# The FFN inputs of a hybrid decoder layer: how their background work is cut into stages

## The chip, the cores and the metric

The kernel is one program on one core of a Trainium2 chip. The metric is the device time in microseconds. Before the change the median of three runs is 2029.3 us (2027.58 to 2030.84).

## The reference, cut to what matters

One layer, 2048 tokens, width 1024, float32:

```
h = rmsnorm(x, norm_mix) * (1 + sc_m) + sh_m
proj = h @ w_in                      # conv mixer and gated mixer, 512 channels each
x = x + g_m * (y_mix @ w_out)        # "out_proj"

h = rmsnorm(x, norm_ffn) * (1 + sc_f) + sh_f       # the FFN inputs
gate, up = split(h @ w_up, 2)        # 1024 -> 2 x 2816
x = x + g_f * ((silu(gate) * up) @ w_down)
y = rmsnorm(x, norm_final)
```

The change concerns the second `h` alone, that is how and when it is computed.

## The kernel before, in words

Channels lie on the 128 partitions and tokens along the rows. The 2048 tokens are four quarters of 512; two quarters make a half, b = 0 or 1. A float32 product is three matmuls on TensorE (PE): each operand is split into a high and a low part, by a copy on ScalarE (ACT, L151) and a subtraction on VectorE (DVE, L152).

Order of the work: half 0 through both mixers and out_proj; half 1 through the convolution mixer (`restart`), the gated mixer (`mixer`) and out_proj; then the FFN's up projection for half 0 and half 1 (`ups`); then the down projection (`down`).

Both FFN projections use a scheme with seven products in place of eight on 2x2 blocks. The right operands of the up projection are therefore not `h` but seven arrays: B11, B21, B22 (quarters and halves of the channels of `h`), and the differences T1 = B12 - B11, T2 = B22 - T1, T3 = T2 - B11, T4 = B21 - T2. `ffn_inputs(b)` makes them in the background of other work, in four passes over kt (128 channels each, from the first and the second half of the channels). It is a generator: each `next()` runs it to its next `yield`, and whoever calls `next()` decides where its instructions stand in the program. A pass reads four tiles of x from DRAM (`xd`), multiplies each by the reciprocal root mean square on GpSimd (POOL, L478), applies gain and shift on ACT (L479, in place), forms four differences on POOL (L494, L500, L506, L508), and stores seven tiles to DRAM (`hd`, L465). A store is put on a list and issued by the next `late.flush()`, behind the latest weight load on the DMA queue. All DMAs are issued by SyncE (SP), in order.

Background work of half 0 runs under `restart` and `mixer` of half 1 (`step()` there is a `next()`), of half 1 under `ups` for half 0. Under `ups` for half 1 the background is `down_sums`, which is not changed.

`ups` walks over 11 pairs of column tiles for each half. A pair has seven products in the order P1, P5, P6, P2, P7, P3, P4 (k = 0 to 6), each of two units of 12 matmuls, so 24 matmuls. After product k the program makes one of the next pair's weights (`weights`: DMA `raw_gu`, POOL differences L595, L596, L599, L604, then the split of A or ws), at k = 0 the POOL sums of the pair before (L678, L680), at k = 3 and k = 5 its stores (L674) with the differences L686 and L687, and in the slots k = 2 and k = 5 one `next()` of the background. The PSUM bank `a` of a unit is used by P1 (copied out by ACT, `s` L628), P6 (`u` L628), P7 (added to `c` by DVE, L647) and P4, each of which begins when the one before has been read out. `s` is then finished after P2 by a sum on DVE (L643) and Silu on ACT (L644).

The background of half 0's `ups` begins with `finish_rms` (eight matmul records `ms` on PE, L146, and the reciprocal root on ACT and DVE), which needs the last squares of out_proj (`sq`, L439), and goes on with `ffn_inputs(1)`.

What the program's order means: a planner orders the instructions of each engine ahead of time, by its own estimate of durations, the earlier in the program first where several are ready. On the chip each engine runs its list in that order, and an instruction that waits holds all that stand behind it on its engine. The pool of [128, 512] tiles (`tmp`) has 17 slots, shared by all of this.

Of the kernel before, what the change touches and what calls it, by code (L numbers as in the profile page):

```python
# [42 lines left out]
def trunk_kernel(  # L43
# [31 lines left out]
    def panel(name, shape, dt=F32R):  # L75
        return pool.tile(shape, dt, tag="panel", name=name, bufs=14)
# [13 lines left out]
    def tmp(name):  # L90
        return tmx(name)[:, :Q]
# [114 lines left out]
    def more_modulation(n):  # L206
        for _ in range(min(n, len(todo))):
            t = todo.pop(0)
            raw = rawslot(f"wm_{t}")
            nc.sync.dma_start(raw, wmodT[t - 16])  # L210
            modulation(t, raw)
            if 32 <= t < 40:
                gains(1, V_NFFN, t - 32)
# [109 lines left out]
    def token_rms(t, name):  # L323

        n = Q // P
        ms = pool.tile([P, n], F32, tag="ms", name=f"ms_{name}", bufs=1)
        for c in range(n):
            sq = tmp(f"sq_{name}")
            nc.scalar.activation(sq, t[:, c, :], AF.Square, accum_out=ms[:, c:c + 1])
        nc.vector.tensor_scalar_mul(ms, ms, 1.0 / CW)  # L330
        r = pool.tile([P, n], F32, tag="rt", name=f"rt_{name}", bufs=2)
        rsqrt_into(r, ms, n)
        return r

    def token_major(u0, hqs, outs, name, after=lambda kt: None):

        pss = [[ps_tile(f"{name}_{i}_{c}") for c in range(Q // P)] for i in range(len(hqs))]
        for kt in range(KT):
            if kt % 2 == 0:
                ws = halves(u0 + kt // 2, f"{name}_{kt // 2}")  # L340
            w = ws[kt % 2]
            for i, hq in enumerate(hqs):
                for c in range(Q // P):
                    csl = slice(c * P, c * P + P)
                    mm3(pss[i][c], hq[kt][:, 0, csl], hq[kt][:, 1, csl], w[:, 0, :], w[:, 1, :],
                        kt == 0, kt == KT - 1)
            after(kt)
        for i, out in enumerate(outs):
            for c in range(Q // P):
                nc.scalar.activation(out[:, c, :], pss[i][c], AF.Gelu_apprx_tanh)  # L350
# [20 lines left out]
    def channel_major(y, name):  # L371
        out = hi_lo_views(f"yb_{name}", CT)
        for ct in range(CT):
            ps = ps_tile(f"tr_{name}_{ct}")
            for c in range(Q // P):
                csl = slice(c * P, c * P + P)
                nc.tensor.transpose(ps[:, csl], y[:, c, ct * P:ct * P + P], ident)
            scaled_split(out[ct], ps, vcol(V_ONB + ct))
        return out
# [8 lines left out]
    def mixer(b, hT, conv, ws_sb, step):  # L388


        vn = [panel(f"v_{b}_{i}", [P, 4, Q], F32) for i in range(QB)]
        token_major(U_V, hT, vn, f"v{b}", lambda kt: (more_modulation(2), step()))
        for i in range(QB):
            conv.normalise(i)
        for i, v in enumerate(vn):
            r = token_rms(v, f"v{b}_{i}")
            for c in range(Q // P):
                nc.vector.scalar_tensor_tensor(
                    out=v[:, c, :], in0=v[:, c, :], scalar=r[:, c:c + 1], in1=vn_b, op0=ALU.mult, op1=ALU.mult
                )  # L400
        us = [panel(f"u_{b}_{i}", [P, 4, Q], F32) for i in range(QB)]
        y = []
        token_major(U_U, hT[:1], us[:1], f"u{b}_0", lambda kt: (more_modulation(1), step()))
        spatial_gate(us[0], vn[0], ws_sb, f"{b}_0")
        y.append(conv.split(0))

        def after(kt):
            step()
            if kt == 5:
                y[0] += channel_major(us[0], f"{b}_0")  # L410

        token_major(U_U, hT[1:], us[1:], f"u{b}_1", after)
        spatial_gate(us[1], vn[1], ws_sb, f"{b}_1")
        y.append(conv.split(1))
        return y, lambda: channel_major(us[1], f"{b}_1")
# [37 lines left out]
    class Late:  # L453
# [5 lines left out]
        def put(self, dst, t):  # L459
            self.stores.append((dst, t))  # L460
# [7 lines left out]
    def ffn_inputs(b):  # L468

        late = Late()  # L470

        def put(name, kt, t):
            late.put(hd[b][name][:, kt, :], t)

        def get(i, kt):
            t = tmp(f"b_{b}_{i}_{kt}")
            nc.sync.dma_start(t, xd[b][kt // 2][:, 2 * (kt % 2) + i, :])
            nc.gpsimd.tensor_mul(t, t, rs[i])  # L478
            nc.scalar.activation(  # L479
                t, t, AF.Identity, bias=mod[:, 24 + kt:25 + kt], scale=gain[:, 1, kt:kt + 1]  # L480
            )
            return t

        rs = [tmp(f"r_{b}_{i}") for i in range(QB)]
        for i in range(QB):
            nc.sync.dma_start(rs[i], rd[b][i])
        yield
        for kt in range(4):
            b11 = get(0, kt)
            put("B11", kt, b11)  # L490
            t1 = get(1, kt)
            yield
            late.flush()
            nc.gpsimd.tensor_sub(t1, t1, b11)  # L494
            put("T1", kt, t1)
            t2 = get(1, kt + 4)
            put("B22", kt, t2)
            yield
            late.flush()
            nc.gpsimd.tensor_sub(t2, t2, t1)  # L500
            put("T2", kt, t2)
            b21 = get(0, kt + 4)
            put("B21", kt, b21)
            yield
            late.flush()
            nc.gpsimd.tensor_sub(b11, t2, b11)  # L506
            put("T3", kt, b11)
            nc.gpsimd.tensor_sub(b21, b21, t2)  # L508
            put("T4", kt, b21)
            yield  # L510
            late.flush()

    def down_sums():

# [27 lines left out]


    ORDER_UP = ("P1", "P5", "P6", "P2", "P7", "P3", "P4")
    ORDER_DOWN = ("P1", "P6", "P7", "P4", "P5", "P3", "P2")

    class Panel:
# [17 lines left out]
        def steps(self):  # L565
            for p in ORDER_UP:
                self.load(RIGHT[p])
                yield
                self.split(RIGHT[p])
                yield  # L570
# [122 lines left out]
    def ups(panels, begin, backgrounds):  # L693


        todo = [(b, p) for b in range(NB) for p in range(NPR)]
        pair, before = begin, None
        for n, (b, p) in enumerate(todo):
            after = Pair(*todo[n + 1], panels[todo[n + 1][0]].t) if n + 1 < len(todo) else None
            bg = backgrounds[b]  # L700
            due = pair.due
            for k, prod in enumerate(ORDER_UP):
                ins = pair.product(prod)
                with tc.issue_after(ins):
                    if k == 0 and due:
                        pair.weights(due)
                    if k and after:
                        after.weights(ORDER_UP[k - 1])
                if p == NPR - 1 and b + 1 < NB:
                    if k:  # L710
                        panels[b + 1].split(RIGHT[ORDER_UP[k - 1]])
                    panels[b + 1].load(RIGHT[prod])
                elif p == 0 and b and k == 0:
                    panels[b].split(RIGHT[ORDER_UP[-1]])
                if before:
                    if k == 0:
                        before.sums()
                    if k == 3:
                        with tc.issue_after(last["load"]):
                            before.stores()  # L720
                    if k == 5:
                        with tc.issue_after(last["load"]):
                            before.last_stores()
                if k in (2, 5):
                    next(bg, None)
            if after:
                after.due = ORDER_UP[-1]
            if p == NPR - 1:
                for _ in bg:
                    pass  # L730
            before, pair = pair, after
        return before

    def down(last_pair):
# [40 lines left out]
        last_pair.last_stores()  # L775
        for prod in ORDER_DOWN[:-1]:
            first = prod in ("P1", "P5")
# [203 lines left out]
    def stepper(g, n=1):  # L981
        return lambda: [next(g, None) for _ in range(n)]

    hT, conv, ws_sb = start()
    y, late = mixer(0, hT, conv, ws_sb, lambda: None)
    hT = []
    g = prepare(1, hT)
# [3 lines left out]
    g = ffn_inputs(0)  # L991
    step = stepper(g)
    restart_step = lambda: None if late_rms else step()
    hT, conv, ws_sb = restart(1, hT, restart_step)
    y, late = mixer(1, hT, conv, ws_sb, step)
    for _ in g:
        pass
    panels = [Panel(b) for b in range(NB)]
# [1 line left out]
    def begin():  # L1000
        yield from panels[0].steps()

    g = begin()
# [74 lines left out]
```

## Time and profile before

| | |
|---|---|
| median of three runs | 2029.3 us |
| the profiled execution's own time | 2028.27 us |
| its span (first to last instruction) | 2026.3 us |
| PE busy | 1956.1 us, 97% of the span |
| DVE, ACT, POOL busy | 57%, 39%, 31% |
| granted PE clock, mean | 0.988 of full speed |

The page gives busy times by engine over the whole span. Matmuls overlap in the pipeline: one takes some 390 ns in the records, and the next begins some 230 ns after it began. What a stage costs is therefore seen in the number of matmuls in a window and in the gaps between them. Rows of a timeline have the start in us, the duration, engine, line and operation, what it writes and reads, and in brackets how long the engine stood idle before it and what released it. A row of windows gives the stretch, its length, the busy us and the number of instructions of PE, PEld (weight loads), DVE, ACT and POOL, the granted PE clock, the busy share of the DMA engines and GB/s.

### The profile page before, as it was taken

To read this page: it belongs to the slowest core of one execution; us is meant where nothing else is said; L and a number is where in the kernel's file an instruction comes from. 1 tells how busy PE (TensorE), PEld (TensorE's weight loads), DVE (VectorE), ACT (ScalarE), POOL (GpSimd) and SP (SyncE) were. 2 spreads that over 40 slices of the span, in tenths; PEclk is the share of its full clock that TensorE was granted. 3 is DMA by queue.
4 is the path that set the end of the run, shared out by engine and by line. 5 is a ranking of instruction groups with operands and counts; after the bars stand their busy time and mean duration, and the time that the engine had idled before them with its cause. 6 is when DMAs were issued, how large, how long until landed. Compare 5 with 4: busy or idle time off the path is not lost.

```text
span 2026.3 us, 23006 instructions
## 1 busy us (share of the span) xinstructions
PE 1956.1 (97%) x8424; PEld 1585.4 (78%) x8424; DVE 1156.8 (57%) x1595; ACT 787.6 (39%) x1314; POOL 636.3 (31%) x440
## 2 busy tenths in 40 slices
PE   5989998999999999999999999999999999999996
PEld 3878876788888877777878888888888888888874
DVE  7988667443287664455454855465454454454464
ACT  3442656322465443333343633333333332333221
POOL 3200025001510235655654475565463100011011
PEclk9999999999999999999999999999999999999998
DMA  8568354332547534334433754543556974243332
GB/s 280 183 204 274 102 189 151 99 120 73 187 141 243 178 102 148 135 110 144 162 110 114 240 171 136 187 161 121 178 172 216 357 261 139 95 150 113 132 120 83
DMA packets 136915, 328.21 MB, mean 162 GB/s; under 512 B 14305, under 2 KB 22497, under 8 KB 134498
## 3 DMA queue, kind: packets, MB, share of 16 engines
q1 hardware_dynamic: 136802, 326.74, 47.2%
q8 instruction: 66, 1.08, 0.2%
q14 instruction: 47, 0.39, 0.1%
HBM read 242.28 MB, written 84.41 MB: 161 GB/s over the span
## 4 chain that ended last, share of the span: by engine, by line
PE 68%; DMA 4%; DVE 4%; POOL 3%; issue 2%; ACT 2%; SPq 0%; DVEq 0%; POOLq 0%; ACTq 0%
PE d_P L174 7%; PE d_P L175 7%; PE d_P L173 7%; PE gu_a L173 7%; PE gu_a L174 6%; PE gu_a L175 6%; DMA raw_gu<-in_wts 3%; PE gu_d L173 3%; PE gu_d L174 3%; PE gu_d L175 3%; PE c L173 2%; PE c L174 2%; PE c L175 2%; PE o L175 1%; PE gu_e L175 1%
## 5 line engine op out<-in xcount | busy, mean ns | idle before, releaser
L152 DVE TENSOR_TENSOR ws<-raw_gu,ws 128x512 fp32r<-128x512 f32 x176 | 197.3, 1159 | 158.7 <-ACT ws L151 150.7
L152 DVE TENSOR_TENSOR A<-raw_gu,A 128x512 fp32r<-128x512 f32 x132 | 101.3, 799 | 122.4 <-ACT A L151 121.5
L151 ACT CAST ws<-raw_gu 128x512 fp32r<-128x512 f32 x176 | 101.8, 616 | 146.0 <-PE gu_d L175 64.8
L595 POOL TENSOR_TENSOR raw_gu<-raw_gu 128x512 f32<-128x512 f32 x44 | 59.1, 1343 | 289.9 <-DMA raw_gu<-in_wts 250.5
L173 PE MATMUL gu_a<-T,ws 128*128 128x512 f32 x352 | 140.3, 399 | 3.4 <-ACT s L628 3.4
L174 PE MATMUL gu_a<-T,ws 128*128 128x512 f32 x352 | 140.0, 398 | 0.0
L175 PE MATMUL gu_a<-T,ws 128*128 128x512 f32 x352 | 139.8, 397 | 0.0
L133 POOL TENSOR_TENSOR sf<-sf,sq 128x512 f32<-128x512 f32 x18 | 28.3, 1576 | 327.2 <-DMA raw_S_d<-sd 226.0
L175 PE MATMUL c<-h,w_c 128*128 128x512 f32 x320 | 125.8, 393 | 4.8 <-DVE w_c L152 4.8
L173 PE MATMUL c<-h,w_c 128*128 128x512 f32 x320 | 126.1, 394 | 0.4 <-DVE ya L301 0.4
L174 PE MATMUL c<-h,w_c 128*128 128x512 f32 x320 | 125.6, 392 | 0.4 <-DVE h L224 0.4
L173 PE MATMUL d_P<-T_d,S_d 128*128 128x512 f32 x264 | 102.7, 389 | 0.0
L174 PE MATMUL d_P<-T_d,S_d 128*128 128x512 f32 x264 | 102.7, 389 | 0.0
L175 PE MATMUL d_P<-T_d,S_d 128*128 128x512 f32 x264 | 102.7, 389 | 0.0
L478 POOL TENSOR_TENSOR b<-b,r 128x512 f32<-128x512 f32 x32 | 42.2, 1334 | 182.4 <-DMA b<-xd 156.9
L151 ACT CAST A<-raw_gu 128x512 fp32r<-128x512 f32 x132 | 78.9, 621 | 45.8 <-PE gu_e L175 23.6
L133 POOL TENSOR_TENSOR sx<-sx,sq 128x512 f32<-128x512 f32 x14 | 21.0, 1498 | 233.1 <-ACT sq L132 232.2
L152 DVE TENSOR_TENSOR S_d<-raw_S_d,S_d 128x512 fp32r<-128x512 f32 x44 | 32.1, 734 | 96.8 <-ACT S_d L151 94.8
L173 PEld LDWEIGHTS gu_a<-T,ws 128*128 128x128 f32 x352 | 66.6, 189 | 20.1 <-ACT s L628 3.9
L174 PEld LDWEIGHTS gu_a<-T,ws 128*128 128x128 f32 x352 | 66.7, 189 | 16.3
L175 PEld LDWEIGHTS gu_a<-T,ws 128*128 128x128 f32 x352 | 66.5, 189 | 16.4
L151 ACT CAST S_d<-raw_S_d 128x512 fp32r<-128x512 f32 x44 | 27.3, 620 | 131.7 <-PE d_P L175 117.8
(256 smaller groups left out, 5571.2 us busy)
## 6 DMA issues: line engine op xcount, KB each, us to landing
raw_gu<-in_wts SPq DMA_DIRECT2D x88, 512.0 KB, 4.2
raw_T_d<-gd_T SPq DMA_DIRECT2D x44, 512.0 KB, 3.7
raw_B_d<-gd_B SPq DMA_DIRECT2D x33, 512.0 KB, 3.7
wm<-in_wmodT SPq DMA_DIRECT2D x32, 512.0 KB, 4.4
raw_o<-in_wts SPq DMA_DIRECT2D x32, 512.0 KB, 5.3
raw_c<-in_wts SPq DMA_DIRECT2D x28, 512.0 KB, 4.2
gd_B<-s SPq DMA_DIRECT2D x44, 256.0 KB, 7.0
gd_T<-s SPq DMA_DIRECT2D x44, 256.0 KB, 2.5
```

What stands on the lines that cost most here:

```text
L133: (add or nc.vector).tensor_add(acc, acc, sq)
L151: nc.scalar.copy(dst[:, 0, :], src)
L152: (sub or nc.vector).tensor_sub(dst[:, 1, :], src, dst[:, 0, :].bitcast(F32))
L173: nc.tensor.matmul(ps, l_hi, r_hi, start=start, stop=False, skip_group_check=onto)
L174: nc.tensor.matmul(ps, l_hi, r_lo, start=False, stop=False, skip_group_check=onto)
L175: nc.tensor.matmul(ps, l_lo, r_hi, start=False, stop=stop, skip_group_check=onto)
L478: nc.gpsimd.tensor_mul(t, t, rs[i])
L595: nc.gpsimd.tensor_add(a21, a21, a22)
```

## The change

`ffn_inputs` is cut into nine stages a pass in place of four. A tile is loaded in one stage, multiplied by the reciprocal root in the next (`scale`, POOL), shifted in the one after (`shift`, ACT), and then enters a difference; the four differences stand in four stages. Under `ups` for half 0 the background gets the slots k = 1, 2, 4 and 5 of a pair in place of 2 and 5; under `mixer` of half 1 it gets two `next()` at each step in place of one. The arithmetic and the numbers of instructions and DMAs stay as they were. The first `next()` under `ups`, which runs `finish_rms`, now stands after P5 in place of P6.

```diff
--- before.py
+++ after.py
@@ -475,40 +475,59 @@
         def get(i, kt):
             t = tmp(f"b_{b}_{i}_{kt}")
             nc.sync.dma_start(t, xd[b][kt // 2][:, 2 * (kt % 2) + i, :])
+            return t
+
+        def scale(i, t):
             nc.gpsimd.tensor_mul(t, t, rs[i])
+
+        def shift(kt, t):
             nc.scalar.activation(
                 t, t, AF.Identity, bias=mod[:, 24 + kt:25 + kt], scale=gain[:, 1, kt:kt + 1]
             )
-            return t
 
         rs = [tmp(f"r_{b}_{i}") for i in range(QB)]
         for i in range(QB):
             nc.sync.dma_start(rs[i], rd[b][i])
         yield
         for kt in range(4):
-            b11 = get(0, kt)
+            late.flush()
+            b11, t1 = get(0, kt), get(1, kt)
+            yield
+            scale(0, b11)
+            scale(1, t1)
+            yield
+            shift(kt, b11)
+            shift(kt, t1)
             put("B11", kt, b11)
-            t1 = get(1, kt)
+            t2 = get(1, kt + 4)
             yield
             late.flush()
             nc.gpsimd.tensor_sub(t1, t1, b11)
             put("T1", kt, t1)
-            t2 = get(1, kt + 4)
+            scale(1, t2)
+            yield
+            late.flush()
+            shift(kt + 4, t2)
             put("B22", kt, t2)
+            b21 = get(0, kt + 4)
             yield
             late.flush()
+            scale(0, b21)
+            yield
+            shift(kt + 4, b21)
+            put("B21", kt, b21)
             nc.gpsimd.tensor_sub(t2, t2, t1)
             put("T2", kt, t2)
-            b21 = get(0, kt + 4)
-            put("B21", kt, b21)
             yield
             late.flush()
             nc.gpsimd.tensor_sub(b11, t2, b11)
             put("T3", kt, b11)
+            yield
+            late.flush()
             nc.gpsimd.tensor_sub(b21, b21, t2)
             put("T4", kt, b21)
             yield
-            late.flush()
+        late.flush()
 
     def down_sums():
 
@@ -542,6 +561,7 @@
 
 
     ORDER_UP = ("P1", "P5", "P6", "P2", "P7", "P3", "P4")
+    BACKGROUND_0, BACKGROUND_1 = (1, 2, 4, 5), (2, 5)
     ORDER_DOWN = ("P1", "P6", "P7", "P4", "P5", "P3", "P2")
 
     class Panel:
@@ -721,7 +741,7 @@
                     if k == 5:
                         with tc.issue_after(last["load"]):
                             before.last_stores()
-                if k in (2, 5):
+                if k in (BACKGROUND_0, BACKGROUND_1)[b]:
                     next(bg, None)
             if after:
                 after.due = ORDER_UP[-1]
@@ -992,7 +1012,7 @@
     step = stepper(g)
     restart_step = lambda: None if late_rms else step()
     hT, conv, ws_sb = restart(1, hT, restart_step)
-    y, late = mixer(1, hT, conv, ws_sb, step)
+    y, late = mixer(1, hT, conv, ws_sb, stepper(g, 2))
     for _ in g:
         pass
     panels = [Panel(b) for b in range(NB)]
```

## Rows read from the trace of the kernel before

**Rows 1.** The page: PE's busy time, share of the span, instructions
```profile
PE 1956.1 (97%) x8424; PEld 1585.4 (78%) x8424; DVE 1156.8 (57%) x1595; ACT 787.6 (39%) x1314; POOL 636.3 (31%) x440
```
**Rows 2.** Windows: restart and mixer; ups of half 0, then half 1
```profile
410.00:650.00 240.00, 240.00 (x1068) 197.47 (x1067) 129.01 (x215) 107.60 (x188) 44.63 (x32) 1.00 0.44 148
...
776.00:1055.00 279.00, 272.04 (x1167) 219.21 (x1167) 138.89 (x171) 106.25 (x185) 154.21 (x111) 0.99 0.39 135
1240.00:1519.00 279.00, 279.00 (x1212) 227.09 (x1211) 151.12 (x174) 98.53 (x175) 167.31 (x119) 1.00 0.47 159
```
**Rows 3.** Waits of PE, 690 to 1130: us in total, times, longest
```profile
PE gu_a L173 <- DVE c L647: 7.0, 6, 1.8
PE gu_a L173 <- ACT s L628: 3.4, 1, 3.4
```
**Rows 4.** Timeline of PE: the longest of the six waits and after it
```profile
781.72 0.50 PE L173 MATMUL gu_a<-T,A 128*128 128x512 f32 x1 [1.79 <-DVE c L647]
...
783.22 0.63 PE L173 MATMUL gu_a<-T,A 128*128 128x512 f32 x1
```
**Rows 5.** Timelines of SP, POOL, ACT and DVE ahead of the last wait
```profile
1007.87 2.03 SPq L674 DMA_DIRECT2D gd_T<-s  x2
1009.95 0.42 SPq L477 DMA_DIRECT2D b<-xd  x1
...
1013.86 2.54 POOL L478 TENSOR_TENSOR b<-b,r 128x512 f32<-128x512 f32 x2 [1.81 <-DMA b<-xd]
...
1009.02 0.63 ACT L644 ACTIVATE s<-s 128x512 f32<-128x512 f32 x1 [1.26 <-DVE s L643]
1015.19 0.82 ACT L479 ACTIVATE b<-b,mod,gain 128x512 f32<-128x512 f32 x1 [5.53 <-POOL b L478]
1016.43 0.81 ACT L479 ACTIVATE b<-b,mod,gain 128x512 f32<-128x512 f32 x1 [0.43 <-POOL b L478]
...
1017.66 0.63 ACT L644 ACTIVATE s<-s 128x512 f32<-128x512 f32 x1
...
1021.63 1.27 DVE L647 TENSOR_TENSOR c<-gu_a,c 128x512 f32<-128x512 f32 x2
```
**Rows 6.** The same places a pair later, without background: ACT, DVE, PE
```profile
1049.35 0.63 ACT L644 ACTIVATE s<-s 128x512 f32<-128x512 f32 x1 [1.23 <-DVE s L643]
...
1050.95 0.63 ACT L644 ACTIVATE s<-s 128x512 f32<-128x512 f32 x1
...
1054.56 0.68 DVE L647 TENSOR_TENSOR c<-gu_a,c 128x512 f32<-128x512 f32 x1
...
1061.22 0.39 PE L173 MATMUL gu_a<-T,A 128*128 128x512 f32 x1
```
**Rows 7.** Waits of ACT from 735 to 1055, largest
```profile
ACT b L479 <- POOL b L478: 52.2, 13, 7.3
```
**Rows 8.** The background's tiles b: landing of their DMAs
```profile
DMA to landing us min/median/max: 2.0/3.4/8.0
```
**Rows 9.** Timelines of PE and ACT in the first pair
```profile
708.85 0.39 PE L175 MATMUL gu_d<-T,ws 128*128 128x512 f32 x1
712.69 0.79 PE L173 MATMUL gu_a<-T,ws 128*128 128x512 f32 x1 [3.45 <-ACT s L628]
...
720.96 1.02 PE L146 MATMUL ms<-s,ones_d 128*128 128x512 f32 x2
...
723.99 0.79 PE L173 MATMUL gu_e<-B,A 128*128 128x512 f32 x1
...
711.53 0.63 ACT L439 ACTIVATE sq<-x 128x512 f32<-128x512 f32 x1 [2.56 <-DVE x L431]
712.07 1.05 ACT L628 COPY s<-gu_a 128x512 f32<-128x512 f32 x2
```
**Rows 10.** Timeline of DVE: the same four operations beside POOL and alone
```profile
583.41 5.03 DVE L319 SCALAR_TENSOR_TENSOR ya<-ya,vec,ya 128x512 fp32r<-128x512 f32 x4
...
610.42 2.73 DVE L319 SCALAR_TENSOR_TENSOR ya<-ya,vec,ya 128x512 fp32r<-128x512 f32 x4
```

More of the change, by code (lines that the diff above doesn't have):

```diff
@@ L495, in ffn_inputs @@
             put("T1", kt, t1)
-            t2 = get(1, kt + 4)
-            put("B22", kt, t2)
+            scale(1, t2)
             yield
             late.flush()
+            shift(kt + 4, t2)
+            put("B22", kt, t2)
+            b21 = get(0, kt + 4)
[5 more added lines that the diff above has]
+            put("B21", kt, b21)
             nc.gpsimd.tensor_sub(t2, t2, t1)
             put("T2", kt, t2)
-            b21 = get(0, kt + 4)
-            put("B21", kt, b21)
             yield
```

## Prediction

> **What bounds the kernel now.** I read the page first. PE is busy for 97% of the span, and the next engine, DVE, for 57% [rows 1]: only what frees PE, or makes it wait, can move the time. The windows by stage come next, because PE's share is a mean. From 410 to 650 us, where the inputs of half 0 are made in the background, PE is busy for 240.00 of 240 us. In the up projection it is busy for 272.04 of 279 us in half 0, with 1167 matmuls, and for 279.00 of 279 us in half 1, with 1212 [rows 2]. The two halves run the same products, and half 1 has a background on POOL too (167 us busy there, 154 us here). The difference, 45 matmuls at 279/1212 = 0.230 us, is 10.4 us. So the stage has about 10 us to give, and I ask which wait ends last there.
>
> The waits of PE name it: six of 1.8 us at most, 7.0 us in all, on `c` L647, and one of 3.4 us on `s` L628 [rows 3]. The first kind stands ahead of P4, which may not write bank `a` before DVE has added P7's result to `c`. I follow one back through the engines. SP issues the load of `b` at 1009.95, behind two stores that waited for POOL [rows 5]. POOL waits another 1.81 us for its landing and multiplies two tiles from 1013.86. ACT has the shift of these tiles (L479) in its list between the Silus of the two units, and stands 5.53 us idle ahead of the first shift and 0.43 us ahead of the second. The second Silu begins 1017.66 - 1009.02 = 8.64 us after the first; a pair later, without background, it is 1050.95 - 1049.35 = 1.60 us [rows 6]. So ACT comes 7.0 us late, and with it the casts behind the Silu, the subtractions that need them on DVE, and `c` L647 behind those. Without background `c` of the first unit is done at 1054.56 + 0.68 = 1055.24, and P4 begins at 1061.22: 5.98 us to spare [rows 6]. 7.0 late against 6.0 spare is a wait of about 1 us; the trace has 1.33 there. ACT waits for L478 thirteen times in these pairs, 52.2 us in all, 7.3 at most [rows 7]; PE feels only what goes beyond the 6 us.
>
> **The stalls ahead of P4.** What the six cost is more than their idle time. The next matmul begins 0.23 us after one began, but idle time counts from its modelled end, 0.39 us after: 0.16 each, 0.96 us. The first matmul after a stall takes 0.50 us, not 0.39 [rows 4]: 0.66 us for six. After the longest, 1.79 us, the records from 783.22 on show eight matmuls of about 0.63 us, 0.43 us apart in place of 0.23, as at the lower (1.2 GHz) of the clock's two levels: eight times 0.20 = 1.6 us. Together 7.0 + 0.96 + 0.66 + 1.6 = 10.2 us, which agrees with the 10.4 us from the windows.
>
> The change takes away what makes ACT wait. The load now stands a slot ahead of its product, and the product a slot ahead of its shift. Two neighbouring slots (k = 1 and 2, or 4 and 5) are a product of 24 matmuls apart, 24 x 0.230 = 5.5 us; from 2 to 4 and from 5 to the next 1 it is 11 us. A load lands after 2.0 to 8.0 us, median 3.4 [rows 8], so in most slots it is there, and otherwise POOL waits some 2.5 us. A shift that finds its product done costs ACT its own 0.82 us, two of them 1.6 us, against the 5.98 us to spare. Queued behind a shift on ACT are the Silu L644, the casts of ws and through them DVE's `c` L647 and P4; behind a product on POOL are the weight differences; behind a load on SP the weight loads and stores. The number of loads (16), products, shifts, differences and stores (28) does not change.
>
> Where is the product only one short slot ahead of its shift? Counting nine stages a pass through slots 1, 2, 4, 5, with the first `next()` on the rms and the loads of r: three fall on k = 2, ahead of the Silu, with their products at k = 1, behind the POOL differences of the next weights (pairs 1, 5 and 6, counted from 0, one of them the double shift); three more fall on k = 5, behind the Silu. I leave 1 us of stall for these three. Bounds: at best all 10.4 us go; at worst ACT waits there as now in more pairs, which is the slower rival below. I take 10.2 - 1.0 = 9.2 us gained.
>
> **The first pair.** P6 follows P5 there after 3.45 us of idle time, because `s` L628 stands on ACT behind the last square of out_proj (L439), which itself waited for DVE [rows 9]. P6 then runs from 712.69 to 720.96, 8.27 us against 5.5, with its first half at the lower clock, and the eight `ms` records follow until 723.99. The change puts `finish_rms` in the slot after P5, so that the `ms` records fall into the gap. P5's last matmul leaves at 708.85 + 0.23 = 709.08. The eight records are 0.43 us apart: 3.03 us from the first to the start of P2, whose first matmul takes 0.79 us and so carries the last of them, 3.4 us in all [rows 9]. Six of them need nothing new: 709.08 + 2.6 = 711.7. The last two need L439, done at 711.53 + 0.63 = 712.16, so they end near 713.0. P6 starts there, `s` being ready at 712.6, now after a gap of some 0.5 us; five of the six stalls above, up to 1.69 us, left the clock at its upper level. With 5.5 us and a slow first matmul (0.4) P2 begins near 719.0 in place of 723.99: 5.0 us. If the clock drops all the same, 2.7 of these remain lost. If the planner leaves `ms` behind P6, or something else arrives late, the term is 0. I take 5.0, since L439 stands ahead of `s` on ACT's list already, so the planner counts the squares as ready by then. Behind `finish_rms` on DVE are eight operations for the two reciprocal roots; they move ahead with it and so come no later against `c` L647 than now.
>
> **Half 0's inputs under the mixer.** PE has no idle time there, so nothing can be gained. Of 38 `next()` (1 + 4 x 9 stages and the last flush) six come in `restart` and 32 in the mixer at two a step, which is all of `v` (16) and the first `u` (16). The last two passes thus lie beside the busiest stretch of DVE, where two passes' worth of sums now may run. DVE beside POOL: four operations took 5.03 us at 583.41 and 2.73 us at 610.42 without POOL [rows 10], 0.57 us more each. If 14 POOL operations of about 1.3 us fall there, they cover 18 us, in which DVE does 14 operations and loses 14 x 0.57 = 8 us; PE waits for that only beyond the lead of the weights. The bounds are 0 and 8 us; I take 0, as the nearest row has it: POOL runs beside these operations now, and PE shows no gap [rows 2].
>
> The Trainium skill has a rule against this part (SBUF — State Buffer, "Who interferes with whom"): a VectorE instruction with two SBUF inputs and a GpSimd one that reads SBUF exclude each other for the whole instruction, whichever is second waits. The 1.26 us against 0.68 us of rows 10 agree with it; by the rule each of the 14 could push DVE by its full 1.3 us, 18 us, an estimate that the sum does without.
>
> **Sum.** 2028.3 us of the profiled execution - 9.2 - 5.0 = 2014.1. The median of the runs is 1.0 us above the profiled one, so 2015 us.
>
> **Rivals.**
> First pair unchanged. `ms` moves but P6 still waits for `s`, or the clock drops, or a weight comes late and gives the 5 us back. For it: DVE and ACT are crowded there, and the gap has its cause in them. Against: P6 needs nothing else. 2015 + 5 = 2020.
>
> The wait moves only. POOL's list is late on the chip because of weight landings, so the shift still stands before its product and half of the stalls stay: 2020, or 2025 with the first pair unchanged. For it: POOL was 1.81 us idle for the load in rows 5 but the whole wait of ACT was 5.53 us, so most of it was POOL being busy, not the load. Against: a slot of 5.5 us more covers that.
>
> DVE in the mixer. The 8 us above come through to PE: 2015 + 8 = 2023.
>
> Slower. Shifts now stand in four slots of a pair, at k = 2 ahead of the Silu as before and at k = 1, 4 and 5 too; if each pair has a shift that stands on ACT more than 5.98 - 1.6 = 4.3 us for its product, every pair of half 0 stalls like the longest now: 1.79 + 0.16 + 0.11 + 1.6 = 3.7 us, nine times 33 us, less the 10.2 of today and 5: 2029 + 18 = 2047. It decides from 4.3 us of wait on. For it: thirteen waits of 4 us on average today. Against: those have product and shift in one slot.
>
> **How the numbers follow.** My forecast 0.50 (its own range 2010 to 2019); first pair unchanged 0.18; the wait moves only 0.17; mixer 0.08; slower 0.07. A difference of 0.2% (4 us) is about what can be told from none. Faster: 0.50 + 0.18 + 0.14 of the moved wait, less 0.03 for mishaps: 0.79; same, 2025 to 2033: 0.12; slower: 0.09. The range 2010 to 2026 leaves out the slower cases and the worst of the moved wait.
>
> **What would show it.** Right: ACT's wait for L478 falls from 52 us to under 15; PE's waits on `c` L647 go or stay below 1.5 us in all; the window of half 0's up projection holds some 1210 matmuls in 279 us; the `ms` records stand between P5 and P6, and P2 of the first pair begins some 5 us nearer to P5's end; PE remains gapless in restart and mixer. Wrong: waits of PE on `c` as large as now, a new wait on ws or A there, or gaps of PE under the mixer.

## The result, and the profile after

The changed kernel takes 2017.68 us (median of four runs, 2015.71 to 2019.45); the kernel before, run beside it, 2028.44 us (2026.32 to 2030.84). The ratio is 0.9943, with a 95% interval from 0.9931 to 0.9956: faster by about 11 us. The profiled execution took 2017.61 us, its span is 2015.9 us. The time lies inside the predicted range, near its middle. The terms of the sum came out unequally, and the mechanism of the largest was not the one predicted.

In the changed kernel the load `get` is L477, the product `scale` L481, the shift L484, the four differences L505, L519, L523, L527, the copy of `s` L648, the Silu L664, the sum on `c` L667.

The page, PE's row and its neighbours [rows 1]; then the windows of [rows 2], the same three stretches:

```profile
PE 1951.1 (97%) x8424; PEld 1583.6 (79%) x8424; DVE 1153.5 (57%) x1595; ACT 786.8 (39%) x1314; POOL 633.7 (31%) x440
```
```profile
410.00:650.00 240.00, 237.94 (x1050) 195.44 (x1049) 121.70 (x208) 103.88 (x181) 42.47 (x32) 0.99 0.43 146
776.00:1055.00 279.00, 277.28 (x1203) 224.97 (x1202) 137.68 (x175) 106.14 (x188) 152.60 (x112) 1.00 0.39 132
1240.00:1519.00 279.00, 279.00 (x1212) 227.00 (x1212) 150.21 (x175) 98.65 (x174) 166.62 (x117) 1.00 0.45 156
```

Half 0's up projection holds 36 matmuls more in the same 279 us: 36 x 0.230 = 8.3 us. It lacks 9 of half 1's 1212. The first row is new: restart and mixer, gapless before, now hold 18 matmuls fewer, 18 x 0.230 = 4.1 us. PE's waits from 400 to 1160 us (us in total, times, longest) give both places, and ACT's largest wait from 735 to 1055 us stands as it was [rows 7]:

```profile
PE u L174 <- DVE w_u L152: 2.1, 1, 2.1
PE gu_a L173 <- DVE c L667: 1.7, 2, 0.9
```
```profile
ACT b L484 <- POOL b L481: 51.5, 15, 7.4
```

PE waits on `c` twice in place of six times, for 1.7 us in place of 7.0, and for `s` no more [rows 3]. Yet ACT waits for POOL's products as long as before, 51.5 us against 52.2.

Three landmarks on PE's timeline split the gain: the first matmul of out_proj of half 1 (609.03 before), P2 of the first pair [rows 9: 723.99 before], and P4 of the eleventh pair (1138.66 before):

```profile
613.74 0.58 PE L173 MATMUL o<-ya,w_o 128*128 128x512 f32 x1
...
722.82 0.39 PE L173 MATMUL gu_e<-B,A 128*128 128x512 f32 x1
...
1129.02 0.39 PE L173 MATMUL gu_a<-T,A 128*128 128x512 f32 x1
```

The kernel is 4.7 us behind when out_proj begins (0.7 of it from ahead of restart, so 4.0 from the mixer), 1.2 ahead at P2 (5.9 from the first pair), 9.6 ahead at the eleventh pair's P4 (8.5 from the pairs). The span is 10.4 us shorter; the last 0.8 us come behind the last product of the down projection.

### The profile page after: what moved, and what is told of

Same layout as the page of the kernel before. It is cut to its first block, busy times and chain, and to the rows that moved or that the text cites. A ratio compares the mean times of both kernels' runs of the same rounds, so it can differ in the third digit from the quotient of the medians.

```text
span 2015.9 us, 23007 instructions
## 1 busy us (share of the span) xinstructions
PE 1951.1 (97%) x8424; PEld 1583.6 (79%) x8424; DVE 1153.5 (57%) x1595; ACT 786.8 (39%) x1314; POOL 633.7 (31%) x440
## 4 chain that ended last, share of the span: by engine, by line
PE 61%; DVE 4%; DMA 3%; POOL 1%; issue 1%; ACT 1%; SPq 0%; DVEq 0%; POOLq 0%; ACTq 0%
PE gu_a L173 7%; PE gu_a L174 7%; PE gu_a L175 7%; PE d_P L173 7%; PE d_P L174 7%; PE d_P L175 7%; PE gu_d L173 4%; PE gu_d L174 4%; PE gu_d L175 4%; PE gu_e L175 2%; PE gu_e L174 2%; PE gu_e L173 2%; DMA raw_gu<-in_wts 1%; DMA raw_T<-hd_T 1%; DVE x L870 0%
## 5 line engine op out<-in xcount | busy, mean ns | idle before, releaser
L615 POOL TENSOR_TENSOR raw_gu<-raw_gu 128x512 f32<-128x512 f32 x44 | 59.5, 1353 | 289.6 <-DMA raw_gu<-in_wts 257.5
L481 POOL TENSOR_TENSOR b<-b,r 128x512 f32<-128x512 f32 x32 | 43.5, 1379 | 185.8 <-DVE ya L301 87.8
L624 POOL TENSOR_TENSOR raw_gu<-raw_gu 128x512 f32<-128x512 f32 x44 | 63.8, 1468 | 41.4 <-DVE A L152 41.4
```

The lines of the kernel that those rows point to most:

```text
L615: nc.gpsimd.tensor_add(a21, a21, a22)
L624: nc.gpsimd.tensor_sub(a12, a12, a11)
```

## The experiments

Each was timed in five rounds beside the kernel before; medians on one chip can be set side by side, ratios across chips.

| kernel | median us | ratio to before | 95% |
|---|---|---|---|
| first chip (before 2029.15): e1_old_half0 | 2015.08 | 0.9936 | 0.9924 to 0.9948 |
| e2_rms_only | 2024.45 | 0.9981 | 0.9968 to 0.9993 |
| e3_two_slots | 2022.82 | 0.9970 | 0.9959 to 0.9982 |
| e5_late_slots | 2014.96 | 0.9939 | 0.9926 to 0.9952 |
| second chip (before 2029.71): e4_after_again | 2019.46 | 0.9949 | 0.9936 to 0.9962 |
| e6_before_late | 2015.81 | 0.9931 | 0.9918 to 0.9944 |
| e7_before_late_rms | 2011.97 | 0.9914 | 0.9901 to 0.9928 |
| e8_sums_later | 2024.57 | 0.9979 | 0.9968 to 0.9990 |
| third chip (before 2029.93): e9_mixer_four | 2021.29 | 0.9958 | 0.9942 to 0.9973 |
| e10_stages_late | 2011.70 | 0.9910 | 0.9896 to 0.9925 |
| e11_before_late_rms_again | 2012.05 | 0.9916 | 0.9901 to 0.9930 |

**e1_old_half0: does the mixer's loss come from the new stages?** The changed kernel, with half 0's inputs made by the four-stage generator of before, one `next()` a step:

```diff
-    g = ffn_inputs(0)
+    g = ffn_inputs_4(0)
...
-    y, late = mixer(1, hT, conv, ws_sb, stepper(g, 2))
+    y, late = mixer(1, hT, conv, ws_sb, step)
```

> The changed kernel with half 0's inputs made as before (four stages a pass, one next() a step in the mixer); half 1 as changed. Theory M: the mixer's part of the change costs PE time, 4.0 us by the two traces (out_proj of half 1 begins 613.74 - 609.03 - 0.7 us later, after a wait of PE of 2.1 us on w_u L152 that was not there before). Then this runs 4.0 us faster than the changed kernel, near 2013.7, and PE has no wait on w_u. Rival N: the loss there is given back later (the first pair waits for work that is as late either way), and this stays within 1 us of the changed kernel, near 2017.5.

The wait on `w_u` is gone. From the matmul that follows the `ms` records in `restart` (413.36 before) to the first of out_proj, PE takes 195.7 us in all eight traces with four stages for half 0, and 199.0 to 200.2 us in the four with nine stages and two `next()` a step: the new stages cost the mixer 3.3 to 4.6 us. Little of that shows in the time here. P4 of the first pair begins 5.1 us earlier than after the change (734.36 against 739.46), but PE was 2.1 us earlier already at the `ms` records of `restart`, ahead of all that the edit moves. Then PE waits 0.7 us for the last square in the first pair and three times on `c`, 3.1 us in all, in place of twice for 1.7. At the eleventh pair's P4 3.5 us are left, 1.4 without the 2.1 (e10 comes back to this). The result lies between the two expectations, and its ratio, 0.9936, is within the intervals of the changed kernel's (0.9943, and 0.9949 in e4).

**e2_rms_only: what the first pair's edit is worth alone.** The kernel before, with the first `next()` moved from P6 to P5:

```diff
-                if k in (2, 5):
+                if k in ((1, 5) if n == 0 else (2, 5)):
```

> The kernel before with one edit: the first next() under the up projection, which runs finish_rms, stands after P5 of the first pair in place of P6. Theory F: the eight ms records fill the gap that PE had there; 6.3 us by the traces, so near 2022, with the six waits on c L647 as before (7 us). Rival: the pairs that follow are supplied by engines that don't come sooner, and what the first pair wins is lost in longer waits on c: near 2028.

By the medians 4.7 us, by the ratio 3.9: between the two expectations and nearer the first. The wait for `s` is gone (0.6 us for the last square in its place), and the waits on `c` grew to 8.3 us from 7.0: there too a part is given back.

**e3_two_slots: stages in the two old slots.** The changed kernel, with two stages at a time in k = 2 and 5 (the first `next()` stays behind P5):

```diff
-                if k in (BACKGROUND_0, BACKGROUND_1)[b]:
+                if b:
+                    times = int(k in (2, 5))
+                elif n == 0:
+                    times = {1: 1, 2: 1, 5: 2}.get(k, 0)
+                else:
+                    times = 2 * int(k in (2, 5))
+                for _ in range(times):
                     next(bg, None)
```

> The changed kernel with the same nine stages a pass, but two stages together in the slots k = 2 and 5 of a pair, in place of one each in 1, 2, 4 and 5 (the first next() stays after P5). Theory A (as predicted): product and shift must stand in different slots; here half of them share one, ACT stands before the shift as it did in the kernel before and the six waits on c L647 come back: 2017.7 + 8 = 2026. Theory B: the planner puts a shift between the two Silus wherever the stages stand, ACT waits some 50 us in either kernel, and what ended the stalls is which work of POOL lies beside DVE's subtractions and how many pairs have such a shift: then this stays near the changed kernel, 2017 to 2021.

It fell between the two. Waits on `c` are 4.9 us in four, nearer to the 7.0 of before than to 1.7, though every product is still a stage ahead of its shift. The slots matter. The trace shows two causes that the next runs take apart: where PE waits, the second Silu comes 8.6 to 9.8 us behind the first, and in the fourth pair T2 and T3 run on POOL beside DVE's `ws` subtractions (1.16 and 1.75 us, alone 0.69), for the longest wait, 2.42 us.

**e5_late_slots: ACT's list itself.** The changed kernel, with the slots k = 0, 4, 5 and 6 (in the first pair 1, 4, 5 and 6), and each shift tied behind the latest Silu of `s` in ACT's list, which `last["silu"]` holds:

```diff
-    BACKGROUND_0, BACKGROUND_1 = (1, 2, 4, 5), (2, 5)
+    BACKGROUND_0, BACKGROUND_1 = (0, 4, 5, 6), (2, 5)
...
+            with tc.issue_after(last["silu"]) if "silu" in last else nullcontext():
+                nc.scalar.activation(
+                    t, t, AF.Identity, bias=mod[:, 24 + kt:25 + kt], scale=gain[:, 1, kt:kt + 1]
+                )
```

> The changed kernel with half 1's background in the slots k = 0, 4, 5 and 6 (first next() after P5 as now), and each shift tied behind the latest Silu of s on ACT's list, so that none can stand between the two Silus of a pair. Theory B: the shift between the Silus is what makes the Silu late; here the second Silu follows the first by 1 to 2 us in every pair, c is done 4 to 6 us ahead of P4, the last two waits of PE on c (1.7 us idle, some 2.3 us with what follows) go, and the time is near 2015.4. Theory A: the slots of the change took the cause away already and the two waits left have another one: no change, 2017.7.

PE no longer waits on `c`. The sixth pair on ACT and PE:

```profile
921.60 0.63 ACT L665 ACTIVATE s<-s 128x512 f32<-128x512 f32 x1 [1.17 <-DVE s L664]
923.26 0.63 ACT L665 ACTIVATE s<-s 128x512 f32<-128x512 f32 x1
924.83 2.31 ACT L485 ACTIVATE b<-b,mod,gain 128x512 f32<-128x512 f32 x3
...
933.53 0.39 PE L173 MATMUL gu_a<-T,A 128*128 128x512 f32 x1
```

The second Silu follows the first after 1.66 us, and the shifts stand behind both. From the second pair to the tenth the Silus are 1.05 to 1.96 us apart, and `c` is done 5.4 to 7.2 us ahead of P4. The time, 2014.96 us, is near the 2015.4 of theory B, but its ratio alone (0.9939, beside 0.9943 and 0.9949) does not exclude theory A; the waits do.

**e6_before_late and e7_before_late_rms: late shifts without the stages.** The kernel before, four stages and two slots, moved from k = 2 and 5 to 4 and 6 from the second pair on, with the same tie; e7 also moves the first pair's two slots to k = 1 and 4, so that `finish_rms` stands after P5 as in e2:

```diff
+            with tc.issue_after(last["silu"]) if "silu" in last else nullcontext():
+                nc.scalar.activation(
+                    t, t, AF.Identity, bias=mod[:, 24 + kt:25 + kt], scale=gain[:, 1, kt:kt + 1]
+                )
...
-                if k in (2, 5):
+                if k in ((2, 5) if n == 0 else ((4, 6), (2, 5))[b]):
```

> The kernel before with its four stages a pass and two slots a pair for half 1, but from the second pair on in k = 4 and 6 in place of 2 and 5, and each shift tied behind the latest Silu of s on ACT's list. Load, product and shift stand in one slot, as before. Theory B (the shift between the two Silus is the cause, wherever the stages are cut): the six waits on c go, 9 to 10 us, ratio 0.9953. Theory A (product and shift in one slot make ACT late): the waits stay, 0 to 2 us, ratio 0.999 to 1.000, or they move to the Silu of u.

> The last one with finish_rms after P5 of the first pair as well. If the two gains add (9 to 10 us and 6 us) the ratio is 0.992 to 0.9925, 2013 us, and it beats the changed kernel by 3 to 4 us, since half 0's inputs are untouched. If the first pair's gain is given back where the pairs are supplied too late, it stays at 0.994 to 0.995.

In e6 the only wait of PE from 400 to 1160 us is that for `s` in the first pair; in e7 there is none. The windows of restart with mixer and of half 0's up projection in e7, and ACT's wait for POOL's products in e6 from 735 to 1055 us:

```profile
410.00:650.00 240.00, 240.00 (x1067) 197.58 (x1066) 126.17 (x212) 106.11 (x186) 44.35 (x32) 1.00 0.44 149
776.00:1055.00 279.00, 279.00 (x1213) 227.31 (x1212) 144.14 (x177) 108.20 (x186) 156.16 (x114) 1.00 0.39 134
```
```profile
ACT b L480 <- POOL b L478: 31.1, 16, 5.9
```

ACT waits in sixteen shifts in e6, each with its product in the same stage, and PE feels none of them: they stand behind the Silus. Both gained more than expected: e6 13.9 us by the medians, where 9 to 10 were expected, and e7 is 7.5 us below the changed kernel on the same chip (2011.97 against 2019.46), where 3 to 4 were. By the traces of e4 and e7 3.3 us of this are the mixer's loss, which e7 does not have.

**e8_sums_later: the other half of the lateness.** In the kernel before, in every second of these pairs, T2 and T3 run on POOL just while DVE subtracts for `ws` behind the second Silu. Here they are tied behind the weight difference of P2:

```diff
+            with tc.issue_after(last["s4"]) if "s4" in last else nullcontext():
+                nc.gpsimd.tensor_sub(t2, t2, t1)
...
-                nc.gpsimd.tensor_sub(a12, a12, a11)
+                last["s4"] = nc.gpsimd.tensor_sub(a12, a12, a11).ins
```

> The kernel before with one edit: the differences T2 and T3 are tied behind the pair's last weight difference (S4) on POOL's list, so that they no longer run beside DVE's subtractions of ws ahead of c L647. ACT's list does not change, nor do its waits. Theory P: in pairs 1, 3, 5 and 7, where c came 4.65 us after the second Silu and not 3.1, it now comes 1.5 us sooner; of their waits 1.79 + 1.09 + 1.69 + 1.33 = 5.9 us about 0.5 us stay, PE waits 1.5 to 2 us on c in all and the ratio is 0.996 to 0.997. Rival: DVE's subtractions are slow there for another reason or wait for ACT alone, and nothing changes.

The sixth pair in the kernel before, on ACT, DVE and POOL, and then in e8 on DVE:

```profile
938.61 0.63 ACT L644 ACTIVATE s<-s 128x512 f32<-128x512 f32 x1
939.08 1.29 POOL L500 TENSOR_TENSOR b<-b,b 128x512 f32<-128x512 f32 x1 [1.73 <-DMA hd_B<-b]
939.85 2.76 DVE L152 TENSOR_TENSOR ws<-raw_gu,ws 128x512 fp32r<-128x512 f32 x2 [8.73 <-ACT ws L151]
940.45 1.61 POOL L506 TENSOR_TENSOR b<-b,b 128x512 f32<-128x512 f32 x1
942.53 1.28 DVE L647 TENSOR_TENSOR c<-gu_a,c 128x512 f32<-128x512 f32 x2
```
```profile
940.22 1.29 DVE L152 TENSOR_TENSOR ws<-raw_gu,ws 128x512 fp32r<-128x512 f32 x2 [8.06 <-ACT ws L151]
941.43 1.28 DVE L649 TENSOR_TENSOR c<-gu_a,c 128x512 f32<-128x512 f32 x2
```

Two subtractions take 2.76 us beside POOL and 1.29 us without it, and the four waits of these pairs (numbers 1, 3, 5 and 7, counted from 0) went to zero. In the pairs between, the second Silu now comes 9.5, 11.8 and 9.8 us behind the first (before: 9.5, 9.3 and 8.5), and PE waits 0.72, 2.74 and 0.75 us, in place of 0.42, 0.66 and 0. Hence the gain of some 4 to 5 us instead of the expected 6 to 8. What delays pair 4 so (ACT waits 9.4 us for one product there) is open.

**e4_after_again** and **e11_before_late_rms_again** are the changed kernel and e7 once more, for a comparison on one chip.

> The changed kernel itself, so that the next three stand beside it on one chip. Ratio to the kernel before 0.994 as measured already; on c L647/L667 PE waits about 2 us.

> The kernel with four stages in two late slots, tied shifts and finish_rms after P5 again, beside the others on one chip: 0.991 to 0.992.

**e9_mixer_four: more `next()` under the mixer.** The changed kernel with

```diff
-    y, late = mixer(1, hT, conv, ws_sb, stepper(g, 2))
+    y, late = mixer(1, hT, conv, ws_sb, stepper(g, 4))
```

> The changed kernel with four next() at each step of the mixer in place of two. Theory M: PE's new wait of 2 to 3 us on w_u L152 comes from five tiles of half 0 (in place of two) whose products and shifts are left for the stretch behind the Gelus of the first u, where ACT stands before each shift and the casts of w_u come behind. With four next() the list of ACT has all 16 shifts ahead of that stretch: no wait on w_u there, 3 to 4 us faster than the changed kernel, ratio 0.9925 to 0.9935, as the kernel with half 0 as before. Rival: the stages put more work beside DVE wherever they stand, and the wait on w_u or one on another weight stays: 0.9945.

The expected cure failed. The wait on `w_u` went, but the shifts came earlier in ACT's list, and one now stands there ahead of the Gelus; ACT, then PE:

```profile
555.57 0.82 ACT L484 ACTIVATE b<-b,mod,gain 128x512 f32<-128x512 f32 x1 [7.20 <-POOL b L481]
...
559.92 4.03 ACT L350 ACTIVATE v<-v 128x512 f32<-128x512 f32 x8
...
560.57 3.62 PE L146 MATMUL ms_a<-acc_sa,ones_c 128*128 128x512 f32 x4 [4.36 <-ACT v L350]
```

It is the same mechanism in another place: PE waits 4.4 us because ACT stands 7.20 us at a shift with the Gelus queued behind.

**e10_stages_late: all the cures together.** The changed kernel with e1's half 0 and e5's slots and tie; its two edits are shown there.

> Half 0's inputs as in the kernel before; half 1's inputs in the nine stages of the change, in the slots k = 0, 4, 5 and 6 with the shifts tied behind the latest Silu, finish_rms after P5. Against the kernel with four stages in two slots, the same tie and finish_rms after P5 (0.9914) only the cutting into stages differs. Theory B: it makes no difference once no shift stands between the Silus, 0.991 to 0.992. Theory A: the stages are worth something of their own, 0.990 or less.

0.9910, beside 0.9916 for e11 on the same chip: 0.35 us between medians whose runs spread over 2 to 3 us. With no shift between the Silus, nine stages for half 1 and four give the same time. Against e5, which differs by half 0 alone, e10 is 5.9 us faster by the ratios (0.9910 and 0.9939, the intervals just apart): here the mixer's loss shows in the time.

## Why the prediction came out right, and where it was wrong

The time was right, 2015 against 2017.68. The predicted terms add up to 14.2 us, and the span of the profiled execution fell by 10.4. Of the signs that the prediction named, two came (the window of half 0's up projection holds 1203 matmuls, and the `ms` records stand between P5 and P6), one was just missed (waits on `c` of 1.7 us, where 1.5 was named), and two failed: ACT's wait did not fall, and the mixer is not gapless.

**The step that failed: "The change takes away what makes ACT wait."** The size was near (9.2 us predicted, 8.5 measured), but by luck, as the mechanism was wrong: ACT's wait was to fall from 52 to under 15 us and measured 51.5. The prediction reckoned with the slots in which a stage stands in the program. The planner does not keep a stage to its slot. After the first pair's Silus SP issues three of a pass's loads in one go, and POOL multiplies all three (timeline rows of the changed kernel, SP and POOL):

```profile
734.14 1.34 SPq L477 DMA_DIRECT2D b<-xd  x3
...
737.68 4.70 POOL L481 TENSOR_TENSOR b<-b,r 128x512 f32<-128x512 f32 x3 [1.77 <-DMA b<-xd]
```

The third product belongs to the slot k = 1 of the next pair, behind a P5 that begins at 750.35, and was done by 742.4. No slot stands between the two Silus, which belong to one product, yet shifts still find their place there in ACT's list, with their product late. The load is late as in rows 5: SP issues it behind two stores (L694) whose tiles POOL has just made. The sixth pair after the change, SP, ACT, DVE and PE:

```profile
920.83 3.72 SPq L694 DMA_DIRECT2D gd_T<-s  x2
924.59 0.42 SPq L477 DMA_DIRECT2D b<-xd  x1
...
923.67 0.63 ACT L664 ACTIVATE s<-s 128x512 f32<-128x512 f32 x1 [1.39 <-DVE s L663]
929.50 0.81 ACT L484 ACTIVATE b<-b,mod,gain 128x512 f32<-128x512 f32 x1 [5.19 <-POOL b L481]
930.80 0.81 ACT L484 ACTIVATE b<-b,mod,gain 128x512 f32<-128x512 f32 x1 [0.49 <-POOL b L481]
932.03 0.62 ACT L664 ACTIVATE s<-s 128x512 f32<-128x512 f32 x1
933.27 1.29 DVE L152 TENSOR_TENSOR ws<-raw_gu,ws 128x512 fp32r<-128x512 f32 x2 [8.19 <-ACT ws L151]
934.48 1.28 DVE L667 TENSOR_TENSOR c<-gu_a,c 128x512 f32<-128x512 f32 x2
935.39 0.40 PE L173 MATMUL gu_a<-T,A 128*128 128x512 f32 x1
```

The second Silu comes 8.36 us behind the first, much as the 8.70 us of the same pair before, and yet `c` of the first unit is done 0.2 us ahead of P4 and PE does not wait. Two things made the difference. First, fewer shifts stand between Silus: 8 in pairs 1 to 8, where 11 stood before, none in pairs 6 and 8, and in pairs 3 and 7 the second Silu comes 4.3 us behind the first, which the slack covers (pairs counted from 0; slack is the time by which `c` is done ahead of P4 when nothing delays it). Second, in no pair with a shift between do T2 and T3 still run on POOL beside the `ws` subtractions: 1.29 us above, 2.76 us in the kernel before. That is 1.5 us, as much as the waits of those pairs were (1.09 to 1.79 us); e8 shows this half alone. The prediction had the slack, 5.98 us, but put all the lateness on ACT and none on DVE behind it. DVE's part is hidden there, because the pair of rows 6 has POOL (L599) beside these subtractions too; one pair on, without it, they take 1.30 us and 7.2 us are spare (the kernel before):

```profile
1052.12 2.51 DVE L152 TENSOR_TENSOR ws<-raw_gu,ws 128x512 fp32r<-128x512 f32 x2 [1.21 <-ACT ws L151]
...
1090.85 1.30 DVE L152 TENSOR_TENSOR ws<-raw_gu,ws 128x512 fp32r<-128x512 f32 x2 [1.21 <-ACT ws L151]
```

The rival "the wait moves only" was right about ACT and wrong about PE: what reaches PE is the excess over the slack, and an excess of about 1 us goes with little. That shifts between the Silus are the cause is shown by e5 to e7: with them behind, every wait on `c` goes, with nine stages or with four, while ACT still waits 12.8 us in e5 and 31.1 in e6. Slots and tie were moved together there; that DVE was merely relieved is not the reason, since two `ws` subtractions still take up to 3.1 us beside POOL in e5, and PE does not wait.

**The first pair: right.** 5.0 us predicted, 5.9 measured. The `ms` records stand between P5 and P6, and no gap is left here, where 0.5 us was reckoned; six of the nine other runs with this edit have a wait of 0.6 to 2.1 us there for the last square (2.1 in e4, the changed kernel again). The rows after the change:

```profile
713.56 0.40 PE L175 MATMUL gu_d<-T,ws 128*128 128x512 f32 x1
713.79 1.02 PE L146 MATMUL ms<-s,ones_d 128*128 128x512 f32 x2
...
716.83 0.79 PE L173 MATMUL gu_a<-T,ws 128*128 128x512 f32 x1
```

P6 then takes 5.99 us in place of 8.27 [rows 9], all at the upper level of the clock. Alone the edit brings 4 to 5 us (e2).

**The mixer: a term mis-sized, 0 against 4.0 lost.** Its bounds were 0 and 8 us, but the mechanism named for them was DVE slowed by POOL, and the rows show ACT's list first (SP, POOL, ACT, DVE and PE under the mixer after the change):

```profile
576.95 2.32 SPq L477 DMA_DIRECT2D b<-xd  x5
582.53 5.51 POOL L481 TENSOR_TENSOR b<-b,r 128x512 f32<-128x512 f32 x4 [0.57 <-DMA b<-xd]
583.86 0.81 ACT L484 ACTIVATE b<-b,mod,gain 128x512 f32<-128x512 f32 x1 [0.44 <-POOL b L481]
591.38 0.45 DVE L330 TENSOR_SCALAR ms_y<-ms_y 128x4 f32<-128x4 f32 x1 [5.75 <-ACT sq_y L329]
594.11 1.30 POOL L527 TENSOR_TENSOR b<-b,b 128x512 f32<-128x512 f32 x1 [0.95 <-DMA hd_B<-b]
594.21 1.22 DVE L124 SCALAR_TENSOR_TENSOR rt_y<-a,rt_y 128x4 f32<-128x4 f32 x1
594.71 1.65 ACT L151 CAST w_u<-raw_u 128x512 fp32r<-128x512 f32 x3
598.27 1.88 DVE L152 TENSOR_TENSOR w_u<-raw_u,w_u 128x512 fp32r<-128x512 f32 x3
599.00 0.50 PE L174 MATMUL u<-w_u,h 128*128 128x512 f32 x1 [2.06 <-DVE w_u L152]
600.50 0.63 PE L174 MATMUL u<-w_u,h 128*128 128x512 f32 x1
```

Five loads, five products and five shifts run as one group where before there were two of each, and each shift waits for its product with the squares `sq_y` and the casts of `w_u` behind it. These casts began at 587.81 before and at 594.71 now. DVE stands idle for 5.75 us in this stretch, waiting for ACT, so up to there it was not held by POOL. Behind that, POOL has a share: L124, which the subtractions for `w_u` stand behind in DVE's list, takes 1.22 us beside POOL's L527, and 0.16 us before:

```profile
590.71 0.16 DVE L124 SCALAR_TENSOR_TENSOR rt_y<-a,rt_y 128x4 f32<-128x4 f32 x1
```

That makes `w_u` 1.1 us later, beside 2.06 us that PE waits; no run parts POOL's share from ACT's. Five matmuls at 0.63 us follow, as at the clock's lower level. The rows on the `ws` subtractions, 2.76 us beside POOL and 1.29 us without it, agree with the rule of the Trainium skill (SBUF — State Buffer, "Who interferes with whom") that the two engines exclude each other.

**Open.** Where the planner puts a shift is read from the traces and not explained. The span of e6 is 13.2 us shorter than before, and its lead at the eleventh pair's P4 is 10.6 us. Of the rest, 1.6 us lie in the down projection, behind one wait of PE for `sf` (the kernel before, then e6):

```profile
1936.61 1.81 PE L146 MATMUL ms_f<-sf,ones_d 128*128 128x512 f32 x2 [2.08 <-POOL sf L133]
1939.07 0.63 PE L175 MATMUL d_P<-B_d,A_d 128*128 128x512 f32 x1
...
1926.01 1.13 PE L146 MATMUL ms_f<-sf,ones_d 128*128 128x512 f32 x2 [2.09 <-POOL sf L133]
1927.43 0.39 PE L175 MATMUL d_P<-B_d,A_d 128*128 128x512 f32 x1
```

After the same wait the kernel before goes on at the clock's lower level and e6 at the upper one. Six of the thirteen profiled executions show the lower level there, both of the changed kernel among them; what decides it no run shows. The other 1.0 us lies behind the last product of the down projection.

A part of an earlier gain is given back as waits on `c` (e1, e2). With the shifts behind both Silus it is not: what the first pair brings e7 over e6, 5.8 us at its P4, is still 5.8 at the eleventh pair's, both counted from the start of out_proj. So the give-back needs the shifts between the Silus; that it is slack used up is argued, and not shown.

## What to carry to other kernels

Ask not how far apart two steps stand in the program but where the waiting instruction stands in its engine's list and what is queued behind it: cutting work into stages set a priority here, while an explicit tie behind the Silu set the position, and brought more with the old stages (0.9914 against 0.9949 on one chip, 3.3 us of which are the mixer's loss). A wait reaches the bounding engine only by its excess over the slack, so a change that leaves 51.5 of 52.2 us of waiting may still win most of what there is; the check on a theory is the wait it names, not the time. A stage that is gapless has no margin on record: work regrouped under it needs a price from the list of the engine that runs it.

## What the runs showed that was not expected

Of waits of PE of much the same length some are followed by the lower clock level and others are not: after 1.79 us (before) and 2.06 us (after) the records show 0.63-us matmuls, after 2.99 us at the same place in e4 they stay at 0.39 to 0.40 us until the next operation. The waits for `sf` in the down projection, 2.08 and 2.09 us, differ in the same way. The second surprise is the size of the interference between POOL and DVE: two `ws` subtractions lost 1.47 us (2.76 against 1.29) beside two POOL subtractions of 1.29 and 1.61 us.
